# A two-layer decoder trunk: norm ratio in two parts, a third gate pair plain, the scan's first blocks moved up, the residual added later

## The chip, the core and the metric

The kernel runs on one core of one Trainium2 chip. The metric is the device time of one execution in microseconds (us). The engines are TensorE (PE; its weight loads are PEld), VectorE (DVE), ScalarE (ACT) and GpSimd (POOL); SyncE (SP) issues most transfers and ScalarE the stores of intermediate tensors.

## The reference, cut to what is computed

All is float32: 1024 positions plus 16 meta tokens, width 1024.

```python
h = concat([meta, x])                                     # 1040 x 1024
h = h + mixer_rglru_swa(rmsnorm(h, g0))                   # layer 0: recurrence and window attention
h = h + swiglu(rmsnorm(h, f0), w_gu0, w_down0)
q, k, v, g = split(rmsnorm(h, g1) @ ret_w_in)             # layer 1: retention, 4 heads
for block in blocks:                                      # 9 blocks of 128 positions per head
    o = (q_b @ k_b.T * decay) @ v_b + (q_b * dq) @ state
    state = decay_chunk * state + (k_b * dk).T @ v_b
h = h + (silu(g) * rmsnorm_noaffine(o)) @ ret_w_out
h = h + swiglu(rmsnorm(h, f1), w_gu1, w_down1)
# swiglu: gate, up = split(x @ w_gu); (silu(gate) * up) @ w_down;  d_ff = 2816
```

## The kernel before

**Products.** Each factor is a pair of parts, a rounded high part and the rest. For the moving operand the high part is an ACT cast (`oh`, L782) and the low part a subtraction (`ol`, L783) on DVE or POOL; for weights these are `hi` (L111, ACT) and `lo` (L113). `mm3` issues three matmuls for a product (high by high L160, high by low and low by high L161 and L162). A matrix product works on pairs of 128-wide blocks: `seven` does a 2 by 2 product of blocks in seven block products, for which POOL forms four sums of weight blocks (`S`, L145 to L151) and DVE four differences of the moving blocks (`T`, L777, in `mixed`). `eight` does it plainly, with eight block products and no sums or differences. In layer 0 a product is 520 wide in two chunks of 260; in layer 1 it is 512 wide, for keys and values 520.

**Norms.** The normed input is needed as two halves of the positions (hf 0 and 1). A half's scale is `ratio`: two DVE scalings, five small matmuls with a column of ones (L276) for the mean, a power, DVE diagonals (`dg`, L284), small matmuls that spread them over the partitions (L285) and an ACT copy. It multiplies the products after the matmul, so the matmuls can start before it. All of `ratio` is emitted in one piece.

**The feed-forward part (`ffn`).** It has 11 pairs of 256 columns. For each, a gate product and an up product; pair 0 is done by `eight`, the rest by `seven`. The differences of the input (`late[1]`) are made during pair 0. Each pair's result is stored in seven tensors `hd` by DMAs that ACT issues (L883). Then come the down products, in groups of pairs: 2, 3, 2, 2, 2 in layer 0 and 2, 3, 3, 3 in layer 1. A group loads `hd` (L894), casts it, and does four `seven` (mp 0 to 3), whose results DVE adds onto h (L828). Before group 0's products the residual h is read back from DRAM (`residual`, L752: 16 tiles), and all additions go onto it. The `ol` of a group's first pair is on DVE in group 0, the rest on POOL, and in later groups all of them are on POOL.

**Retention.** The input projection has 24 products of 256 columns: gate pairs 0 and 1 by `eight` (`first8`; `ratio` for both halves is called in pair 0), 4 key and query pairs, 8 value pairs, then gate pairs 2 to 7 by `seven`. Between gate pairs 6 and 7, block 0 of head 0 is prepared (`ahead`: loads, value parts, key transposes L1195). The scan then goes over 36 blocks: `updates`, `ahead` one block further, `outputs`, `state`, and `third` (gating of the block before: `yt`, `yh`). Output products of a half head (`output`) are put between blocks as fills. After the last head's output the residual gets its new value (L1285), and is normed (L762), stored and split for layer 1's feed-forward part.

**Order.** Operations go to the engines in the order that a scheduler makes of the emission order, and each engine takes its own in order. 56 SBUF buffers (`slot`), 18 more (`xslot`, `fslot`, `rslot`) and 8 PSUM banks (`ps` 4, `ax` 4) are handed out as they come free.

Of the kernel before, what the change touches and what calls it, by code (L numbers as in the profile page):

```python
# [71 lines left out]
def tile_hybrid(ctx: ExitStack, tc, hT, wfm, wqkv, wo0, lruw, pk, qkg, ck, c0, ret_tab, ret_m,  # L72
# [193 lines left out]
    def ratio(acc, n, sc, pool):  # L266

# [12 lines left out]
        for c0 in range(0, len(cols), 4):  # L280
            ps = bank()
            for j, (a, w) in enumerate(cols[c0:c0 + 4]):
                dg = stg.tile([P, P], F32, tag="dg", bufs=5, name=nm("dg"))
                nc.vector.tensor_scalar(dg[:w, :w], ident[:w, :w], rc[:w, c0 + j:c0 + j + 1], None, op0=ALU.mult)  # L284
                nc.tensor.matmul(ps[:, j * P:j * P + w], ones[:w, :], dg[:w, :w], start=True, stop=True)  # L285
            a, b = cols[c0][0], min(n, cols[c0][0] + 512)
            nc.scalar.copy(R[:, a:b], ps[:, :b - a])
        return R[:, :n]
# [512 lines left out]
    def eight(u, xs, chunks, evac):  # L801

        last = None
        for m, c in ((1, 1), (2, 1), (1, 2), (2, 2)):
# [5 lines left out]
            if last:  # L810
                evac(*last)
            last = (m, c, [ps[:, :b - a] for ps, (a, b) in zip(bk, chunks)])
        evac(*last)
# [3 lines left out]
    def ffn(fp, wgu, wd, groups, xs, R, n, late, done):  # L817
# [13 lines left out]
        for i in range(NP):  # L831
# [27 lines left out]
            if i == 0:  # L859
                def gate0(m, c, bk):  # L860
                    if (m, c) == (1, 2):
                        R.append(late[0]())
# [9 lines left out]
                eight(unit4(wgu[0]), xs, chunks, gate0)  # L872
                late[1](0, 1)
                eight(unit4(wgu[NP]), xs, chunks, up0)
                late[1](2, 3)
            else:
                seven(unit22(wgu[i], 512, fp), xs, chunks, blocks(gt))
                seven(unit22(wgu[NP + i], 512, fp), xs, chunks, blocks(ut))
# [5 lines left out]
        def residual(mp):  # L884
            for m in (2 * mp, 2 * mp + 1):
                for hf in range(2):
                    h[m][hf] = unspill(m, hf, n, xslot if hf and m >= 4 else None)

        for gi, grp in enumerate(groups):
            xs = [{} for _ in grp]  # L890
            for ki, key in enumerate(MOVING):
                for j, i in enumerate(grp):
                    raw = xslot("raw")[:, :n]
                    nc.sync.dma_start(raw, hd[i][key])  # L894
                    xs[j][key] = hilo(raw, n, slot, nc.gpsimd if gi or j else nc.vector)
                if gi == 0 and ki == 1:
                    residual(0)
            w = len(grp) * P
            for mp in range(4):
                if gi == 0 and mp < 3:  # L900
                    residual(mp + 1)
                h1, h2 = h[2 * mp], h[2 * mp + 1]
                outs = (h1[0], h1[0], h1[1], h2[1], h2[1], h1[1], h2[0])

                def evac(k, bk):
                    each(add, outs[k], bk, outs[k])
# [547 lines left out]
```

## Time and profile before

| | us |
|---|---|
| median of three runs (range) | 2714.45 (2713.97 to 2720.88) |
| the profiled execution | 2718.94 |
| its span, first to last instruction | 2717.2 |
| TensorE busy | 2588.8 |
| VectorE busy | 1819.7 |
| GpSimd busy | 1491.8 |
| ScalarE busy | 1153.4 |

The profiled execution is one of its own; its time is the span and 1.7 us around it. Times in the rows count from the start of the span. A granted clock of 1.00 is TensorE's 2.4 GHz and 0.50 is 1.2 GHz; a stretch in between is a mean of the two. A window's PE busy time is the length less the time in which no matmul ran, whatever the clock. "A <- B" in a list of waits means that A's engine sat idle until B's instruction ended.

### The profile page before, as it was taken

The numbers are of one execution on the slowest core, as the hardware profiler recorded it, in microseconds if no ns is written. First come the engines' busy times: TensorE is split into PE (matmuls) and PEld (weight loads), VectorE is DVE, ScalarE is ACT, GpSimd is POOL, SyncE is SP. The second block draws the span as 40 slices with busy tenths as digits, with TensorE's granted clock in tenths as the row PEclk, the third lists the DMA queues.
The fourth block names the chain that finished last, engine by engine and source line by source line (L and its number), as shares of the span: only waits on it lengthen the run. The fifth ranks groups of instructions, "written<-read, shape, count | busy, mean of one in ns | idle before, by whom it ended". The sixth has DMA issues, their size and how long they took to land.

```text
span 2717.2 us, 43283 instructions
## 1 busy us (share of the span) xinstructions
PE 2588.8 (95%) x15734; PEld 2287.1 (84%) x15734; DVE 1819.7 (67%) x3130; ACT 1153.4 (42%) x2425; POOL 1491.8 (55%) x1358
## 2 busy tenths in 40 slices
PE   8989999999998999889999997999989999998999
PEld 7877989999998999779899875777767788886777
DVE  6977676666666889878844344555588655556875
ACT  4666543333333444332233444555543333334442
POOL 3746234554554867457754444454454655565784
PEclk9999999999999999999999998999999999999999
DMA  4001141223225643323232334343332232226442
GB/s 151 32 27 54 63 165 61 96 102 111 84 105 178 207 123 94 113 78 110 98 102 95 117 107 169 114 134 115 106 128 79 96 112 102 97 93 232 161 150 89
DMA packets 145318, 302.31 MB, mean 111 GB/s; under 512 B 18512, under 2 KB 35408, under 8 KB 145104
## 3 DMA queue, kind: packets, MB, share of 16 engines
q1 hardware_dynamic: 103792, 232.49, 25.6%
q10 hardware_dynamic: 41152, 66.54, 6.6%
q8 instruction: 123, 2.02, 0.3%
q14 instruction: 91, 0.75, 0.1%
q0 software_dynamic: 160, 0.52, 0.1%
HBM read 216.60 MB, written 82.89 MB: 110 GB/s over the span
## 4 chain that ended last, share of the span: by engine, by line
PE 78%; DVE 12%; ACT 3%; issue 3%; POOL 2%; DMA 1%; ACTq 0%; SPq 0%; DVEq 0%; POOLq 0%
PE ps L160 16%; PE ps L162 16%; PE ps L161 16%; PE ax L160 8%; PE ax L161 8%; PE ax L162 8%; DVE lo L113 3%; DVE ol L783 1%; DVE h L828 1%; DVE T L777 1%; PE ps L673 1%; DVE xp L762 1%; POOL ol L783 1%; PE ps L1097 1%; ACT oh L782 1%
## 5 line engine op out<-in xcount | busy, mean ns | idle before, releaser
L160 PE MATMUL ps<-oh,hi 128*128 128x260 f32 (+1 forms) x2160 | 695.2, 324 | 20.9 <-ACT oh L782 10.3
L162 PE MATMUL ps<-oh,lo 128*128 128x260 f32 (+1 forms) x2160 | 691.5, 323 | 12.8 <-DVE lo L113 12.6
L161 PE MATMUL ps<-ol,hi 128*128 128x260 f32 (+1 forms) x2160 | 694.0, 322 | 0.5 <-DVE ol L783 0.5
L160 PE MATMUL ax<-oh,hi 128*128 128x260 f32 (+1 forms) x1652 | 531.1, 324 | 9.5 <-ACT oh L782 3.8
L161 PE MATMUL ax<-ol,hi 128*128 128x260 f32 (+1 forms) x1652 | 532.1, 323 | 5.3 <-DVE ol L783 5.3
L162 PE MATMUL ax<-oh,lo 128*128 128x260 f32 (+1 forms) x1652 | 527.7, 322 | 0.9 <-DVE lo L113 0.9
L113 DVE TENSOR_TENSOR lo<-S,hi 128x512 fp32r<-128x512 f32 (+2 forms) x392 | 342.3, 876 | 212.8 <-ACT hi L111 197.9
L111 ACT CAST hi<-S 128x512 fp32r<-128x512 f32 (+2 forms) x392 | 219.0, 561 | 567.3 <-PE ps L161 251.3
L160 PEld LDWEIGHTS ps<-oh,hi 128*128 128x128 f32 x2160 | 409.4, 190 | 58.7 <-ACT oh L782 11.4
L162 PEld LDWEIGHTS ps<-oh,lo 128*128 128x128 f32 x2160 | 408.4, 190 | 49.3 <-DVE lo L113 16.9
L161 PEld LDWEIGHTS ps<-ol,hi 128*128 128x128 f32 x2160 | 410.4, 190 | 32.9 <-DVE ol L783 1.3
L291 POOL TENSOR_TENSOR t<-t,rf 128x520 f32<-128x520 f32 (+1 forms) x190 | 280.4, 1483 | 118.8 <-DVE t L1027 47.3
L160 PEld LDWEIGHTS ax<-oh,hi 128*128 128x128 f32 x1652 | 313.2, 190 | 37.9 <-ACT oh L782 4.7
L161 PEld LDWEIGHTS ax<-ol,hi 128*128 128x128 f32 x1652 | 313.3, 190 | 31.8 <-DVE ol L783 6.8
L113 DVE TENSOR_TENSOR lo<-raw,hi 128x512 fp32r<-128x512 f32 (+2 forms) x312 | 266.7, 858 | 106.0 <-ACT hi L111 99.1
L162 PEld LDWEIGHTS ax<-oh,lo 128*128 128x128 f32 x1652 | 312.2, 189 | 26.7 <-DVE lo L113 1.6
L111 ACT CAST hi<-raw 128x512 fp32r<-128x512 f32 (+2 forms) x344 | 199.4, 584 | 311.9 <-PE ps L161 188.9
L145 POOL TENSOR_TENSOR S<-rb 128x512 f32<-128x512 f32 (+2 forms) x98 | 115.8, 1182 | 317.5 <-DVE lo L113 286.8
L783 POOL TENSOR_TENSOR ol<-raw,oh 128x520 fp32r<-128x520 f32 (+1 forms) x140 | 202.2, 1471 | 24.5 <-ACT oh L782 10.3
L151 POOL TENSOR_TENSOR S<-raw,S 128x512 f32<-128x512 f32 (+2 forms) x98 | 130.8, 1335 | 80.2 <-DVE lo L113 77.4
L146 POOL TENSOR_TENSOR S<-S,raw 128x512 f32<-128x512 f32 (+2 forms) x98 | 116.0, 1183 | 83.3 <-issue 49.3
L149 POOL TENSOR_TENSOR S<-raw,rb 128x512 f32<-128x512 f32 (+2 forms) x98 | 122.7, 1252 | 52.0 <-DVE lo L113 52.0
(303 smaller groups left out, 4773.6 us busy)
## 6 DMA issues: line engine op xcount, KB each, us to landing
raw<-in_wgu_dram SPq DMA_DIRECT2D x48, 512.0 KB, 3.3
rb<-in_wgu_dram SPq DMA_DIRECT2D x40, 512.0 KB, 3.2
raw<-hd SPq DMA_DIRECT2D x77, 260.0 KB, 3.4
raw<-hd SPq DMA_DIRECT2D x77, 256.0 KB, 3.0
raw<-in_wro_dram SPq DMA_DIRECT2D x32, 512.0 KB, 3.3
raw<-in_wr_dram SPq DMA_DIRECT2D x26, 512.0 KB, 3.3
hd<-T ACTq DMA_DIRECT2D x44, 260.0 KB, 2.7
rb<-in_wr_dram SPq DMA_DIRECT2D x22, 512.0 KB, 3.4
```

Source lines behind the costliest of these rows:

```text
L111: nc.scalar.copy(hi, src)
L113: eng.tensor_tensor(out=lo, in0=src, in1=f32(hi), op=ALU.subtract)
L145: nc.gpsimd.tensor_tensor(out=s1, in0=a21, in1=a22, op=ALU.add)
L146: nc.gpsimd.tensor_tensor(out=s2, in0=s1, in1=a11, op=ALU.subtract)
L149: nc.gpsimd.tensor_tensor(out=s3, in0=a11, in1=a21, op=ALU.subtract)
L151: nc.gpsimd.tensor_tensor(out=s4, in0=a12, in1=s2, op=ALU.subtract)
L160: nc.tensor.matmul(ps, ah, bh, start=first and i == 0, stop=False, skip_group_check=more)
L161: nc.tensor.matmul(ps, ah, bl, start=False, stop=False, skip_group_check=more)
L162: nc.tensor.matmul(ps, al, bh, start=False, stop=last and i == n - 1, skip_group_check=more)
L291: (eng or nc.vector).tensor_tensor(out=out_, in0=a, in1=b, op=ALU.mult)
L673: nc.tensor.matmul(k.po[:n, o:o + 64], sb[:, i * P:(i + 1) * P], vt[:, k.b - len(segs) + 1 + j, g * 64:(g + 1) * 64], start=False, stop=g ...
L783: eng.tensor_tensor(out=lo, in0=src, in1=f32(hi), op=ALU.subtract)
```

## The change

The norm ratio is cut in two: `ratio_begin` (scalings, means, power) returns `finish` (diagonals, their matmuls, the copy). `eight` takes hooks that run behind a given block, and with hooks it holds two blocks back before it evicts, not one. The feed-forward part's gate pair 1 in both layers, and gate pair 2 of retention, go by `eight`. In the down products, group 0's first product onto each h tile is copied by ACT and the others are added, with no residual; the residual is loaded into temporaries and added by DVE behind mp 1 to 3 of group 1 and mp 0 of group 2. The `ol` of every group's first pair is on DVE. In retention, `ahead` works two blocks further; blocks 0 to 2 of head 0 are emitted before gate pair 7, and what depends on the gates follows behind block 4. The norm of the last head's half 0 is put off until the last block's gating is emitted.

```diff
     def ratio(acc, n, sc, pool):
+        return ratio_begin(acc, n, sc, pool)()
+    def ratio_begin(acc, n, sc, pool):
...
-        for c0 in range(0, len(cols), 4):
-            ps = bank()
-            for j, (a, w) in enumerate(cols[c0:c0 + 4]):
-                dg = stg.tile([P, P], F32, tag="dg", bufs=5, name=nm("dg"))
-                nc.vector.tensor_scalar(dg[:w, :w], ident[:w, :w], rc[:w, c0 + j:c0 + j + 1], None, op0=ALU.mult)
-                nc.tensor.matmul(ps[:, j * P:j * P + w], ones[:w, :], dg[:w, :w], start=True, stop=True)
-            a, b = cols[c0][0], min(n, cols[c0][0] + 512)
-            nc.scalar.copy(R[:, a:b], ps[:, :b - a])
-        return R[:, :n]
+        def finish():
+            for c0 in range(0, len(cols), 4):
+                ps = bank()
+                for j, (a, w) in enumerate(cols[c0:c0 + 4]):
+                    dg = stg.tile([P, P], F32, tag="dg", bufs=5, name=nm("dg"))
+                    nc.vector.tensor_scalar(dg[:w, :w], ident[:w, :w], rc[:w, c0 + j:c0 + j + 1], None, op0=ALU.mult)
+                    nc.tensor.matmul(ps[:, j * P:j * P + w], ones[:w, :], dg[:w, :w], start=True, stop=True)
+                a, b = cols[c0][0], min(n, cols[c0][0] + 512)
+                nc.scalar.copy(R[:, a:b], ps[:, :b - a])
+            return R[:, :n]
+        return finish
...
-    def eight(u, xs, chunks, evac):
-        last = None
-        for m, c in ((1, 1), (2, 1), (1, 2), (2, 2)):
+    def eight(u, xs, chunks, evac, hooks={}):
+        wait = []
+        for i, (m, c) in enumerate(((1, 1), (2, 1), (1, 2), (2, 2))):
...
-            if last:
-                evac(*last)
-            last = (m, c, [ps[:, :b - a] for ps, (a, b) in zip(bk, chunks)])
-        evac(*last)
+            if i in hooks:
+                hooks[i]()
+            wait.append((m, c, [ps[:, :b - a] for ps, (a, b) in zip(bk, chunks)]))
+            if len(wait) > (2 if hooks else 1):
+                evac(*wait.pop(0))
+        for w in wait:
+            evac(*w)
...
-            if i == 0:
-                def gate0(m, c, bk):
-                    if (m, c) == (1, 2):
-                        R.append(late[0]())
+            if i < 2:
+                def gate0(m, c, bk, gt=gt):
...
-                eight(unit4(wgu[0]), xs, chunks, gate0)
+            if i == 0:
+                fin = []
+                eight(unit4(wgu[0]), xs, chunks, gate0,
+                      {2: lambda: fin.append(late[0]()), 3: lambda: R.append(fin[0]())})
...
+            elif i == 1:
+                eight(unit4(wgu[i]), xs, chunks, gate0)
...
+            if i:
...
         def residual(mp):
...
-                    h[m][hf] = unspill(m, hf, n, xslot if hf and m >= 4 else None)
+                    t = unspill(m, hf, n)
+                    nc.vector.tensor_tensor(out=h[m][hf][:, :n], in0=h[m][hf][:, :n], in1=t[:, :n], op=ALU.add)
...
         for gi, grp in enumerate(groups):
...
-                    xs[j][key] = hilo(raw, n, slot, nc.gpsimd if gi or j else nc.vector)
-                if gi == 0 and ki == 1:
-                    residual(0)
+                    xs[j][key] = hilo(raw, n, slot, nc.vector if j == 0 else nc.gpsimd)
...
-                if gi == 0 and mp < 3:
-                    residual(mp + 1)
-                h1, h2 = h[2 * mp], h[2 * mp + 1]
-                outs = (h1[0], h1[0], h1[1], h2[1], h2[1], h1[1], h2[0])
+                at = [(2 * mp + r, c) for r, c in ((0, 0), (0, 0), (0, 1), (1, 1), (1, 1), (0, 1), (1, 0))]
...
-                    each(add, outs[k], bk, outs[k])
+                    m, hf = at[k]
+                    if gi == 0 and k in (0, 2, 3, 6):
+                        h[m][hf] = xslot("h") if hf and m >= 4 else slot("h")
+                        each(lambda o, ps: nc.scalar.copy(o, ps), h[m][hf], bk)
+                    else:
+                        each(add, h[m][hf], bk, h[m][hf])
...
                 seven(unit22(wd[gi][mp], w, fp), xs, chunks, evac)
+                if gi == 1 and mp or gi == 2 and not mp:
+                    residual((mp - 1) % 4)
...
     def late0():
-        r = ratio(acc[1], 520, sc[1], fp)
-        products((Rf[0], r), sc)
-        return r
+        finish = ratio_begin(acc[1], 520, sc[1], fp)
+        def run():
+            r = finish()
+            products((Rf[0], r), sc)
+            return r
+        return run
...
-        pend = []
+        pend, temps = [], [slot]
...
-                    t[key] = slot("t")
+                    t[key] = temps[0]("t")
...
         def scaled(chunks, c, t, bk):
...
-                t = slot("t")
+                t = temps[0]("t")
...
         def first8(i, between):
...
-            def evac(m, c, bk):
-                if m == 1 and i == 0:
-                    Rr.append(ratio(acc2[c - 1], 520, tr[c - 1], ap))
-                fin(m - 1, c - 1, None, bk)
-            eight(unit4(wr[8 + i]), xo2, REST, evac)
+            part = []
+            def begin(c):
+                part.append(ratio_begin(acc2[c], 520, tr[c], ap))
+            def end():
+                Rr.append(part.pop(0)())
+            def turn():
+                end()
+                begin(1)
+            eight(unit4(wr[8 + i]), xo2, REST, lambda m, c, bk: fin(m - 1, c - 1, None, bk),
+                  {1: lambda: begin(0), 2: turn, 3: end} if i == 0 else {})
...
+        first8(2, ())
...
-        for i in range(2, 7):
+        for i in range(3, 7):
...
+        def turn(i):
+            k, b = seq[i]
+            if b < 8:
+                updates(k, b)
+            ahead(i + 2)
+            if b:
+                outputs(k, b)
+            if b < 8:
+                state(k, b)
         ahead(0)
+        ahead(1)
+        for i in range(3):
+            turn(i)
+        temps[0] = aslot
         proj7(15, REST, gate(7))
...
+        tail = []
...
         def output(hd, hf, u_, yh, yl):
...
                 if hd == NH - 1:
-                    if m == 0:
-                        acc3[hf] = slot("acc")
-                    xp[m][hf] = normed(m, hf, "g3", 512, tr[hf][:, 8:520], acc3[hf])
-                    spill(m, hf, 0, 512)
-                    plain(xo, xp, m, hf, 512, slot, nc.vector)
+                    def run(m=m):
+                        if m == 0:
+                            acc3[hf] = slot("acc")
+                        xp[m][hf] = normed(m, hf, "g3", 512, tr[hf][:, 8:520], acc3[hf])
+                        spill(m, hf, 0, 512)
+                        plain(xo, xp, m, hf, 512, slot, nc.vector)
+                    tail.append(run)
+                    while hf and tail:
+                        tail.pop(0)()
...
         for i, (k, b) in enumerate(seq):
-            if b < 8:
-                updates(k, b)
-            ahead(i + 1)
-            if b:
-                outputs(k, b)
-            if b < 8:
-                state(k, b)
-            if i and seq[i - 1][1]:
-                third(*seq[i - 1])
-                if seq[i - 1][1] in (4, 8):
-                    k_, hf = seq[i - 1][0], seq[i - 1][1] // 8
-                    fills += [(lambda k_=k_, hf=hf, u_=u_: output(k_.hd, hf, u_, *k_.ys[hf])) for u_ in range(4)]
-            if i == 4:
+            if i > 2:
+                turn(i)
+            for k_, b_ in seq[1:4] if i == 4 else seq[i - 1:i] if i > 4 else ():
+                if not b_:
+                    continue
+                third(k_, b_)
+                if b_ in (4, 8):
+                    fills += [(lambda k_=k_, hf=b_ // 8, u_=u_: output(k_.hd, hf, u_, *k_.ys[hf])) for u_ in range(4)]
+            if i == 5:
...
-            if fills and i not in (32, 33):
+            if fills and i not in (32, 33, 34):
...
+        while tail:
+            tail.pop(0)()
...
-    late = (lambda: ratio(acc3[1], 512, tr[1][:, 8:520], fp), mixes(xo, xp, 512, lambda j: fslot if j < 2 else slot))
+    late = (lambda: ratio_begin(acc3[1], 512, tr[1][:, 8:520], fp), mixes(xo, xp, 512, lambda j: fslot if j < 2 else slot))
```

On TensorE, in retention's gate pair 0, the second half's means stand behind the first half's ratio. Before, the rows from its means (L276) to its diagonals' matmuls (L285) are:

```order
L276 MATMUL ax_14649<-ckt,acc_13748 128x1 x4
L276 MATMUL ax_14649<-ckt,acc_13748 8x1
L160 MATMUL ps_14974<-oh_13744,hi_14942 128x260
L161 MATMUL ps_14974<-ol_13745,hi_14942 128x260
...
L162 MATMUL ps_14974<-oh_14307,lo_14944 128x260
L285 MATMUL ax_14659<-dg_14660,ckt 128x128
L285 MATMUL ax_14659<-dg_14663,ckt 128x128
```

In the kernel after, where `finish` is a function of its own, the same place reads (L280 for the means, L291 for the diagonals):

```order
L291 MATMUL ax_14636<-dg_14637,ckt 128x8
L280 MATMUL ax_14645<-ckt,acc_13777 128x1 x4
L280 MATMUL ax_14645<-ckt,acc_13777 8x1
L160 MATMUL ax_14659<-oh_13783,hi_14525 128x512
L161 MATMUL ax_14659<-ol_13784,hi_14525 128x512
...
L162 MATMUL ps_14983<-oh_13794,lo_14971 128x512
L291 MATMUL ax_14684<-dg_14685,ckt 128x128
L291 MATMUL ax_14684<-dg_14688,ckt 128x128
```

Between the means and the diagonals stood 12 matmuls of 260 columns; now there are 30 of 512 columns.

In SP's queue, at layer 0's first group of down products (`raw` from `hd` is a load of a group, `h` from `keep` one of the residual), it was:

```order
L894 DMA raw_10708<-hd_5626 128x520
L894 DMA raw_10714<-hd_6126 128x520
L752 DMA h_10874<-keep_1913_4854 128x520
L752 DMA h_10878<-keep_1924_4901 128x520
L752 DMA h_11026<-keep_1935_4948 128x520
L752 DMA h_11030<-keep_1946_4995 128x520
L894 DMA raw_11320<-hd_6614 128x520
L894 DMA raw_11326<-hd_7114 128x520
L752 DMA h_10652<-keep_0806_4487 128x520
L752 DMA h_10654<-keep_1859_4633 128x520
L752 DMA h_10656<-keep_0811_4498 128x520
L752 DMA h_10658<-keep_1880_4713 128x520
```

It is now:

```order
L911 DMA raw_10697<-hd_5626 128x520
L911 DMA raw_10703<-hd_6123 128x520
L141 DMA rb_11006<-in_wd_0_dram 128x512
...
L911 DMA raw_11301<-hd_6611 128x520
...
L911 DMA raw_12255<-hd_8119 128x520
L760 DMA h_11799<-keep_0806_4487 128x520
L760 DMA h_11802<-keep_1859_4633 128x520
L911 DMA raw_12261<-hd_8619 128x520
```

The residual's loads have moved from within the loads of group 0 and 1 to behind the loads of group 1 and among those of group 2.

On DVE, at the last head's last block (`yt` is the gating of that block, `xp` and `ol` from it a normed tile of half 0), the rows were:

```order
L762 SCALAR_TENSOR_TENSOR xp_23181<-h_20101,pkt,R_14734 128x512
L1285 TENSOR_TENSOR h_20103<-ps_23202,h_20103 128x512
L783 TENSOR_TENSOR ol_23189<-xp_23181,oh_23188 128x512
L762 SCALAR_TENSOR_TENSOR xp_23216<-h_20103,pkt,R_14734 128x512
L1285 TENSOR_TENSOR h_20105<-ps_23227,h_20105 128x512
L783 TENSOR_TENSOR ol_23224<-xp_23216,oh_23223 128x512
L762 SCALAR_TENSOR_TENSOR xp_23241<-h_20105,pkt,R_14734 128x512
L1285 TENSOR_TENSOR h_20107<-ps_23271,h_20107 128x512
L783 TENSOR_TENSOR ol_23249<-xp_23241,oh_23248 128x512
L291 TENSOR_TENSOR yt_23257<-ax_23252,sg_22969 128x512
```

They are now:

```order
L1332 TENSOR_TENSOR h_20213<-ps_23151,h_20213 128x512
L113 TENSOR_TENSOR lo_23345<-raw_23337,hi_23343 128x512
L1332 TENSOR_TENSOR h_20215<-ps_23184,h_20215 128x512
L299 TENSOR_TENSOR yt_23170<-ax_23165,sg_23005 128x512
L770 SCALAR_TENSOR_TENSOR xp_23251<-h_20207,pkt,R_14763 128x512
L1332 TENSOR_TENSOR h_20217<-ps_23198,h_20217 128x512
L791 TENSOR_TENSOR ol_23257<-xp_23251,oh_23256 128x512
L770 SCALAR_TENSOR_TENSOR xp_23260<-h_20209,pkt,R_14763 128x512
L1332 TENSOR_TENSOR h_20219<-ps_23222,h_20219 128x512
```

The last block's `yt` stands ahead of the first normed tile, where it stood behind six of them.

## Rows read from the trace of the kernel before

**Rows 1.** The page's head, then its busy times: busy us, share, instructions.

```profile
span 2717.2 us, 43283 instructions
...
PE 2588.8 (95%) x15734; PEld 2287.1 (84%) x15734; DVE 1819.7 (67%) x3130; ACT 1153.4 (42%) x2425; POOL 1491.8 (55%) x1358
```

**Rows 2.** The page's chain that ended last, by engine.

```profile
PE 78%; DVE 12%; ACT 3%; issue 3%; POOL 2%; DMA 1%; ACTq 0%; SPq 0%; DVEq 0%; POOLq 0%
```

**Rows 3.** Windows: stretch, length, each engine's busy us (instructions), granted clock, DMA share, GB/s.

```profile
440.00:480.00 40.00, 34.90 (x256) 34.10 (x255) 35.06 (x49) 15.59 (x31) 21.16 (x13) 0.87 0.23 81
520.00:840.00 320.00, 320.00 (x2668) 320.00 (x2667) 206.15 (x295) 118.58 (x239) 165.44 (x119) 1.00 0.27 98
840.00:920.00 80.00, 69.70 (x537) 67.96 (x536) 60.58 (x112) 34.57 (x74) 48.09 (x41) 0.94 0.67 231
920.00:1080.00 160.00, 155.62 (x1288) 154.52 (x1287) 138.34 (x285) 66.10 (x144) 121.86 (x109) 1.00 0.40 118
1120.00:1240.00 120.00, 105.23 (x571) 90.08 (x570) 93.88 (x125) 41.81 (x79) 65.66 (x47) 0.94 0.26 91
1600.00:1720.00 120.00, 103.78 (x437) 80.29 (x436) 57.15 (x101) 57.63 (x126) 53.01 (x57) 0.93 0.44 150
2000.00:2040.00 40.00, 31.67 (x132) 24.96 (x132) 35.47 (x43) 16.07 (x30) 19.36 (x14) 0.87 0.38 138
2080.00:2120.00 40.00, 35.28 (x136) 26.58 (x135) 33.97 (x42) 15.60 (x28) 21.85 (x15) 0.91 0.26 93
2120.00:2440.00 320.00, 320.00 (x1380) 258.87 (x1379) 183.57 (x239) 114.75 (x200) 176.16 (x125) 1.00 0.29 102
2440.00:2560.00 120.00, 110.81 (x456) 85.99 (x455) 90.51 (x125) 50.88 (x102) 84.77 (x67) 0.97 0.62 210
```

**Rows 4.** TensorE's waits, 440 to 520: who waits for whom, total us, times, longest.

```profile
PE ax L161 <- DVE ol L783: 2.7, 1, 2.7
PE ps L162 <- DVE lo L113: 1.6, 1, 1.6
```

**Rows 5.** TensorE's waits, 840 to 920.

```profile
PE ps L160 <- ACT oh L782: 6.1, 1, 6.1
PE ps L160 <- DVE h L828: 2.0, 1, 2.0
```

**Rows 6.** Timeline, 865 to 873: start, us, engine, line, operation, idle before and its end.

```profile
865.04 5.00 SPq L752 DMA_DIRECT2D h<-keep  x4
...
871.65 1.68 ACT L782 CAST oh<-raw 128x520 fp32r<-128x520 f32 x3 [4.72 <-DMA h<-keep]
```

**Rows 7.** TensorE's waits, 1120 to 1240.

```profile
PE ax L285 <- DVE dg L284: 6.1, 2, 3.4
...
PE ps L162 <- DVE lo L113: 4.8, 2, 3.5
...
PE ax L160 <- ACT oh L782: 2.3, 1, 2.3
```

**Rows 8.** TensorE's waits, 1600 to 1720.

```profile
PE ax L160 <- ACT kd L1195: 12.5, 6, 5.9
```

**Rows 9.** Timeline, 2000 to 2010, around the last block of the scan.

```profile
2007.36 0.68 DVE L291 TENSOR_TENSOR yt<-ax,sg 128x512 f32<-128x512 f32 x1
...
2008.85 1.65 PE L160 MATMUL ps<-yh,hi 128*128 128x512 f32 x3 [6.75 <-ACT yh L1248]
```

**Rows 10.** TensorE's waits, 2440 to 2560.

```profile
PE ps L160 <- ACT oh L782: 4.3, 2, 3.4
```

**Rows 11.** Tile h on VectorE, 860 to 1110: count, duration ns min/median/max.

```profile
L828 DVE TENSOR_TENSOR h<-ps,h x153: 409/416/430, 880.7 to 1109.6; 128x260 f32<-128x260 f32 x153
```

**Rows 12.** Tile lo on VectorE, 920 to 1080.

```profile
L113 DVE TENSOR_TENSOR lo<-S,hi x56: 408/558/1664, 919.5 to 1079.8; 128x256 fp32r<-128x256 f32 x40, 128x384 fp32r<-128x384 f32 x16
```

**Rows 13.** Tile ol on VectorE, 440 to 480.

```profile
L783 DVE TENSOR_TENSOR ol<-T,oh x12: 686/692/1822, 441.2 to 470.9; 128x520 fp32r<-128x520 f32 x12
```

**Rows 14.** Tile ol on GpSimd, 900 to 1060.

```profile
L783 POOL TENSOR_TENSOR ol<-raw,oh x52: 1288/1490/1644, 899.4 to 1058.2; 128x520 fp32r<-128x520 f32 x52
```

## The prediction

> **What bounds the kernel now.** I read the busy times first: TensorE is busy for 2588.8 of 2717.2 us [rows 1], and in the chain that ended last it has 78%, DVE 12%, ACT 3% [rows 2]. So the time is TensorE's work plus what it loses, and a change pays only where TensorE waits or runs slowly. Next I read the windows [rows 3]. In undisturbed stretches TensorE does 2668 matmuls of 260 columns in 320 us (0.120 us each) and 1380 of 512 in 320 us (0.232 us each), at a granted clock of 1.00. The lost time is in a few stretches. For each I count the idle time (length less PE busy) and the clock's loss: at a mean granted clock c in a window W, the slow part runs at 1.2 instead of 2.4 GHz, and half of its length is lost, which makes (1-c)W. From rows 3:
>
> - 440 to 480 (layer 0, gate pair 1): 5.1 idle + 0.13x40 = 5.2, so 10.3.
> - 840 to 920 (layer 0, start of the down products): 10.3 + 4.8 = 15.1.
> - 1120 to 1240 (start of retention): 14.8 + 7.2 = 22.0.
> - 1600 to 1720 (start of the scan): 16.2 + 8.4 = 24.6.
> - 2000 to 2040 (the last block): 8.3 + 5.2 = 13.5.
> - 2080 to 2120 (layer 1, gate pair 1): 4.7 + 3.6 = 8.3.
> - 2440 to 2560 (layer 1, start of the down products): 9.2 + 3.6 = 12.8.
>
> Together 106.6 us. In each of these windows the clock is below 1.00 where TensorE had just been idle, so a wait that goes takes its slow stretch along. Last I read who ends the waits in these stretches [rows 4 to 10], and what DVE's and GpSimd's instructions cost [rows 11 to 14].
>
> **What it costs TensorE.** Three products by `eight` instead of `seven` mean one more block product each: 24 matmuls of 260 columns in layer 0, 12 of 512 in retention, 12 of 512 in layer 1. 24x0.120 + 24x0.232 = +8.5 us [rows 3]. Nothing hides these. The two-part ratio, the moved blocks and the late residual add no matmul.
>
> **Gate pair 1, layer 0.** TensorE waits 2.7 us for an `ol` of a difference T and 1.6 us for a `lo` behind it in DVE's queue [rows 4], with DVE busy 35.1 of 40 us [rows 3]. A plain product needs no T: its 192 matmuls (23 us) stand between, and the first T is needed two block products into the up product. Against it: the last four T take their buffers only when the plain product has let go of its own, so that some 5.7 us (48 matmuls) remain for them. I take -8 of the 10.3 (ends 0 and -10.3).
>
> **Layer 1, gate pair 1.** The same with 96 matmuls of 0.232: -7 of 8.3 (ends 0 and -8.3).
>
> **Start of retention.** The wait for the diagonals is 6.1 us in two pieces, the longer 3.4 [rows 7]. The second half's ratio had 12x0.120 = 1.4 us of matmuls to hide behind and gets 30x0.232 = 7.0, so its 2.7 goes. The first half's cover stays (18 matmuls instead of 21), and so does its 3.4. Gate pair 2 by `eight` puts 22 us between the differences T and their first use, so the 3.5 of the 4.8 for `lo` and the 2.3 for `oh` go [rows 7]. With half of the clock's 7.2: -2.7 - 3.5 - 2.3 - 3.6 = -12 (ends -2.7 and -18).
>
> **Start of the scan.** Six waits for `kd`, the scaled keys, make 12.5 us, one of them 5.9 [rows 8]: with one block of look-ahead, block b's chain of loads, transposes and ACT copies isn't done when TensorE asks for it. Now gate pair 7's 84 matmuls (19.5 us) lie among the first blocks' chains. I take two thirds of the waits and half of the 8.4 for the clock: -8 - 4 = -12 (ends 0, if the value loads are late all the same, and -21). For the rest of the scan I take nothing.
>
> **The last block.** TensorE waits 6.75 us for `yh`, ready when `yt` was run by DVE at 2007.36 [rows 9], behind six normed tiles in DVE's queue. They now come later. The normed work isn't gone: it stands beside half 1's 96 output matmuls (22 us), and the plain products of half 0 cover half 1's tiles. -7 of 13.5 (ends +3, if half 1's tiles are then late, and -12).
>
> **First group of the down products.** The wait of 6.1 us is for the first cast of a `raw` [rows 5], which ACT did at 871.65 when transfers of h<-keep had kept its queue waiting for 4.72 us; SP issued the first four at 865.04 [rows 6], in a window where the DMA engines are 0.67 busy [rows 3]. Without these loads I take half of the wait, since the stores of the last pair and the `raw` loads themselves stay: -3. The 2.0 for DVE's h [rows 5] goes, as ACT writes four of seven results. With half of the clock's 4.8: -7.5 (ends -2 and -13). In layer 1, 4.3 us of waits for the same cast [rows 10] fall to 1.5, and half of 3.6 goes: -4.5, of which +1 is given back as below: -3.5.
>
> **Groups 1 and 2, DVE.** This is where the change costs. DVE is busy 138.3 of 160 us there, 34.6 in the 40.3 us (336 matmuls) of a group of two pairs [rows 3]. It gets 7 `ol` more per group, 12 additions of the residual in group 1 and 4 in group 2. The trace has no such addition; the nearest row is `ol` on DVE, 0.69 to 1.82 us, median 0.69 [rows 13], of the same 520 columns and two SBUF inputs. The `lo` subtractions show why it spreads, 0.41 to 1.66 [rows 12], while additions that read PSUM keep to 0.41 to 0.43 [rows 11]: two inputs from SBUF are slow beside GpSimd's work. GpSimd loses 7x1.49 = 10.4 us per group [rows 14], so I take 1.0 us each. Group 1 (three pairs, 60.5 us): 1.5x34.6 + 19 = 71 us. Group 2: 34.6 + 11 = 45.6. Groups 3 and 4: 41.6. That is 10.5 + 5.3 + 2x1.3 = 18 us over TensorE's pace. Some 24 `lo` per group get shorter as GpSimd does less, about 0.1 us each, which takes back 2.4 to 3.6 per group, some 11. I take +6 in layer 0 (ends 0 and +20), and +1 in layer 1, where DVE is busy 90.5 of 120.
>
> **Sum.** What goes: -8 - 7 - 12 - 12 - 7 - 7.5 - 3.5 = -57. Of this I hold back an eighth, as DVE ends 12% of the chain [rows 2] and takes the next place when a wait goes: +7. With +6 and +8.5: -35.5. The profiled execution took 2718.9 us (span and 1.7 around it), 4.5 more than the median of the runs, 2714.45; I put the difference onto the median: 2679.
>
> **Rivals.**
>
> First, the waits at the scan's start and the last block only move: the value loads and DVE's normed tiles are still late by as much. For it: `kd` waits stand behind loads, and DVE is busy 35.5 of 40 us around the last block [rows 3]. Against it: ACT is busy 57.6 of 120 us at the scan's start, so there is room to work ahead. -12 - 7 are then missing: 2698.
>
> Second, slower: DVE bounds the down products. 32 additions and 49 moved `ol` come to DVE. At 1.5 us each, near the upper end of rows 13, the 44 of layer 0 take 66 us with 26 us of room (60.5 - 51.9 and three times 5.7), so 40 over; the 37 of layer 1 take 55 with about 40 of room (58.5 us of matmuls in a group, DVE busy 0.75 of them, three groups), so 15 over. 55 in the place of 7 makes 2679 + 48 = 2727. It decides from about 1.3 us each. For it: DVE's 0.86 share; against it, GpSimd's own load falls.
>
> Third, DVE and GpSimd take turns at one resource, so moving `ol` off GpSimd gives more than it takes: a group of two pairs now has GpSimd's 121.9/4 = 30.5 us and 28 `lo` of 0.41, 42 us of turns in 40.3. In group 2 this becomes 30.5 - 10.4 + 11.5 + 11x0.69 = 39.2. Then the +6 goes and so do some 4 us of small waits there: 2669. The Trainium skill ("GPSIMD Engine Reference", Key points) says that GpSimd shares its SBUF interfaces with VectorE, with contention where a DVE instruction has two SBUF inputs; the trace agrees in the spread of `lo` (0.41 to 1.66) beside additions from PSUM (0.41 to 0.43), but doesn't show whether the two take turns or only slow down. By it alone the time would be 2669.
>
> **How the numbers follow.** The forecast 0.60, with its own range 2660 to 2697; the first rival 0.17; the second 0.10; the third 0.13. A measurement of this kernel can tell about 0.3% (8 us) from no change, so faster means below 2706, and slower above 2722. Faster: 0.57 of the forecast's 0.60, 0.13 of the third rival, 0.11 of the first rival, so 0.81. No change: 0.03 + 0.05 = 0.08. Slower: the second rival and 0.01 of the first, 0.11. The range reaches from 2655 to 2712: some 0.05 are left out below and 0.12 above.
>
> **What would show it.** Right: PE's waits at 440 to 480 and in layer 1's gate pair 1 are gone and the clock is 1.00 there; one wait for diagonals at the start of retention, not two; the wait for `yh` of the last block below 1 us; the first cast of the down products waits for no h. Wrong: waits for `kd` at the scan's start of 8 us or more; DVE busy above 39 of 40 us in groups 1 and 2 with waits of TensorE for h of over 8 us per layer; additions of the residual at 1.3 us or more; the plain products at more than 8.5 us.

## The result and the profile after

The kernel after takes 2698.96 us in the median of its runs, the kernel before 2714.82: a ratio of 0.9938, with an interval of 0.9917 to 0.9959. One of its five runs took 4956 us, in a slow state, and is left out of the ratio. The change is 16 us less where 35.5 were forecast. The profiled execution of the kernel after has a span of 2703.4 us, 13.8 less than before. The page's head, busy times (engine, us, share, instructions) and chain:

```profile
span 2703.4 us, 43322 instructions
PE 2593.5 (96%) x15782; PEld 2296.1 (85%) x15782; DVE 1841.3 (68%) x3154; ACT 1160.5 (43%) x2452; POOL 1404.4 (52%) x1288
...
PE 79%; DVE 12%; ACT 3%; issue 3%; DMA 2%; POOL 1%; SPq 0%; ACTq 0%; DVEq 0%; POOLq 0%
```

TensorE's busy time is up by 4.7 us [rows 1], for 48 matmuls more, and the span is down: less is lost. DVE keeps its 12% of the chain [rows 2]. The windows (stretch, length, busy us of PE, PEld, DVE, ACT, POOL with instructions, granted clock, DMA share, GB/s) are moved to where each stage now lies, and answer to [rows 3]:

```profile
440.00:480.00 40.00, 40.00 (x335) 40.00 (x335) 33.79 (x50) 12.98 (x24) 17.89 (x11) 1.00 0.20 74
836.00:916.00 80.00, 73.36 (x578) 72.10 (x576) 51.67 (x90) 37.53 (x94) 37.65 (x34) 0.96 0.38 122
916.00:1076.00 160.00, 146.53 (x1141) 143.21 (x1139) 146.49 (x281) 68.92 (x145) 93.77 (x80) 0.96 0.51 165
1132.00:1252.00 120.00, 118.66 (x657) 101.57 (x655) 101.00 (x133) 47.03 (x88) 66.48 (x46) 1.00 0.30 108
1593.00:1713.00 120.00, 104.23 (x445) 80.44 (x444) 57.81 (x103) 59.47 (x129) 53.68 (x60) 0.94 0.46 156
1988.00:2028.00 40.00, 39.30 (x177) 31.77 (x176) 36.47 (x46) 17.53 (x32) 19.42 (x13) 1.00 0.35 128
2055.00:2095.00 40.00, 39.70 (x171) 31.84 (x170) 39.76 (x48) 14.68 (x27) 22.80 (x14) 1.00 0.26 93
2410.00:2530.00 120.00, 106.50 (x427) 82.30 (x427) 74.58 (x105) 55.95 (x114) 65.38 (x54) 0.94 0.48 160
```

Reading them as in the prediction (idle time plus (1-c)W): gate pair 1 of layer 0 loses 0 us (was 10.3), the start of retention 1.3 (was 22.0), the scan's start 15.8 + 7.2 = 23.0 (was 24.6), the last block 0.7 (was 13.5), layer 1's gate pair 1 0.3 (was 8.3). The two starts of the down products lose 6.6 + 3.2 = 9.8 (was 15.1) and 13.5 + 7.2 = 20.7 (was 12.8), and the groups behind the first, 916 to 1076, 13.5 + 6.4 = 19.9, where they lost 4.4. TensorE's waits in the whole of layer 0's down products (waiting, waited for, total us, times, longest), of which [rows 5] shows the start, first before (840 to 1126), then after (836 to 1131):

```profile
PE ps L160 <- ACT oh L782: 6.1, 1, 6.1
PE ps L160 <- DVE h L828: 5.0, 5, 2.0
```

```profile
PE ps L160 <- DVE h L840: 10.6, 9, 3.5
PE ax L161 <- DVE ol L791: 3.1, 2, 2.3
PE ps L160 <- ACT oh L790: 2.9, 1, 2.9
```

The first wait for a cast has fallen from 6.1 to 2.9 us as forecast, but the waits for DVE's h have gone from 5.0 to 10.6, and there are 3.1 for `ol`. In layer 1 the waits for the cast, forecast to fall from 4.3 [rows 10] to 1.5, haven't fallen (2410 to 2530):

```profile
PE ps L160 <- ACT oh L790: 4.8, 2, 3.4
```

From one stage's landmark to the next (the last store of a pair, the last addition of a layer's down products, the first addition of an output product), the two profiles differ by -3.9 us up to the down products of layer 0, +15.4 in these, -18.3 up to the first output product, -23.3 from there to the end of layer 1's gate products, and +16.2 in layer 1's down products. So the question was why the down products cost 31 us where -5 was forecast, and why the rest gave 45 where 31 was forecast.

### The profile page after: what moved, and what is told of

It is laid out like the page before. It is cut to its first block, busy times and chain, and to the rows that moved or that the text cites. A ratio compares the mean times of both kernels' runs of the same rounds, so it can differ in the third digit from the quotient of the medians.

```text
span 2703.4 us, 43322 instructions
## 1 busy us (share of the span) xinstructions
PE 2593.5 (96%) x15782; PEld 2296.1 (85%) x15782; DVE 1841.3 (68%) x3154; ACT 1160.5 (43%) x2452; POOL 1404.4 (52%) x1288
## 4 chain that ended last, share of the span: by engine, by line
PE 79%; DVE 12%; ACT 3%; issue 3%; DMA 2%; POOL 1%; SPq 0%; ACTq 0%; DVEq 0%; POOLq 0%
PE ps L160 16%; PE ps L161 16%; PE ps L162 16%; PE ax L160 9%; PE ax L161 9%; PE ax L162 9%; DVE lo L113 2%; DVE ol L791 2%; DVE xp L770 1%; DVE h L840 1%; PE ps L681 1%; DMA raw<-hd 1%; DVE T L785 1%; PE ps L1120 1%; DMA h<-keep 1%
## 5 line engine op out<-in xcount | busy, mean ns | idle before, releaser
L113 DVE TENSOR_TENSOR lo<-S,hi 128x512 fp32r<-128x512 f32 (+2 forms) x380 | 314.1, 828 | 194.8 <-ACT hi L111 181.7
L162 PEld LDWEIGHTS ps<-oh,lo 128*128 128x128 f32 x2160 | 409.1, 190 | 42.0 <-DVE lo L113 10.4
L111 ACT CAST hi<-S 128x512 fp32r<-128x512 f32 (+2 forms) x380 | 212.0, 559 | 523.7 <-PE ps L161 263.8
L113 DVE TENSOR_TENSOR lo<-raw,hi 128x512 fp32r<-128x512 f32 (+2 forms) x318 | 257.4, 813 | 108.3 <-ACT hi L111 100.2
L299 POOL TENSOR_TENSOR t<-t,rf 128x520 f32<-128x520 f32 (+1 forms) x181 | 267.6, 1486 | 112.8 <-DVE t L1050 48.5
L791 POOL TENSOR_TENSOR ol<-raw,oh 128x512 fp32r<-128x512 f32 (+1 forms) x91 | 143.0, 1594 | 19.9 <-ACT oh L790 8.5
```

The source lines that it names most:

```text
L111: nc.scalar.copy(hi, src)
L113: eng.tensor_tensor(out=lo, in0=src, in1=f32(hi), op=ALU.subtract)
L162: nc.tensor.matmul(ps, al, bh, start=False, stop=last and i == n - 1, skip_group_check=more)
L299: (eng or nc.vector).tensor_tensor(out=out_, in0=a, in1=b, op=ALU.mult)
L791: eng.tensor_tensor(out=lo, in0=src, in1=f32(hi), op=ALU.subtract)
```

## The experiments

All times are medians beside runs of the kernel before on the same chip (2716 to 2720 us); a difference under some 4 us between two of them is not told apart.

**The down products alone, both ways.** `e_down_back` is the kernel after with `ffn`'s part from `residual` to the group loop as before; `e_down_alone` is the kernel before with that part as after.

```diff
...
+                if gi == 0 and mp < 3:
+                    residual(mp + 1)
...
-                if gi == 1 and mp or gi == 2 and not mp:
-                    residual((mp - 1) % 4)
```

> The kernel after, with the down products (residual, first products, ol) as in the kernel before. Theory A (the down products cost what was not forecast: +15 us in layer 0 and +16 in layer 1 in the two profiles): 2699 - 31 = 2668 (2660 to 2676). Rival B (the down products only show a delay that comes from elsewhere, such as a later first load): 2690 to 2700.

> The kernel before, with only the down products changed. Theory A: slower by the same 31 us, 2746 (2735 to 2755). Rival B: 2710 to 2720.

Measured: 2663.8 (ratio 0.9811, 0.9796 to 0.9825) and 2742.4 (1.0098, 1.0079 to 1.0116). The down products cost 35 us in the kernel after and 26 in the kernel before. Theory A stands, and `e_down_back` beats both kernels.

**The parts of it.** `e_ol_back` has one line of that part as before, `e_res_back` all of it but that line:

```diff
-                    xs[j][key] = hilo(raw, n, slot, nc.vector if j == 0 else nc.gpsimd)
+                    xs[j][key] = hilo(raw, n, slot, nc.gpsimd if gi or j else nc.vector)
```

> The kernel after, with only the ol of groups 1 and up on GpSimd again (the late residual stays). Theory A1 (VectorE's load in groups 1 and 2 is what costs, the ol with 28 x 1.16 + 21 x 1.26 = 59 us being more of it than the 32 additions with 30 us): 2699 - 18 = 2681 (2675 to 2688). Rival A2 (the additions cost, since they stand in VectorE's queue and wait for their loads): 2694 to 2702. Third theory (VectorE and GpSimd take turns, so that ol on GpSimd is dearer): 2702 to 2715.

> The kernel after, with the residual loaded ahead of group 0 and all results added on VectorE as before, but the ol of every group's first pair on VectorE as after. Theory A1: the ol still cost about 18 and group 0's waits come back: 2685 (2678 to 2692). Rival A2 (the additions and their loads are the cost): 2668 to 2676.

Measured: 2694.6 and 2688.6. The first lies in A2's range and the second in A1's, so neither theory holds alone: the one half gives back 4.4 of the 35, the other 10.3. The other way round, `e_res_back` differs from `e_down_back` by `ol` on VectorE alone, and that costs 24.9 us (2688.6 - 2663.8). TensorE's waits for VectorE in layer 0's down products (860 to 1130), in `e_down_back` and in `e_res_back`:

```profile
PE ps L160 <- DVE h L840: 5.0, 5, 2.0
```

```profile
PE ps L160 <- DVE h L840: 13.1, 11, 2.6
```

So the price of a part depends on what else is in the kernel.

`e_no_res` is the kernel after without the call of `residual`, `e_no_res_ol` without that and with the `ol` line as before:

> The kernel after without the residual in both feed-forward parts (loads and 32 additions are left out, so the output lacks it); the ol stay on VectorE. It shows what the additions and their loads cost where they now stand. Theory A1 (VectorE's queue is the bound in groups 1 and 2): 2699 - 20 = 2679 (2670 to 2686), since the ol alone still cost 10 to 15. Rival A3 (the copies by ScalarE in group 0 are the cost, as they delay its casts): 2692 to 2700.

> The kernel after with the ol on GpSimd in groups 1 and up, and without the residual in both feed-forward parts (loads and 32 additions left out, so the output lacks it). What is left of the change in the down products is ScalarE's copies in group 0 and the loads that are gone from it. Theory A1 (VectorE's extra work is all that costs): faster than the kernel after with the down products as before (2663.8), by group 0's waits for the residual: 2655 (2650 to 2660). Rival A3 (ScalarE's copies delay its casts and hold PSUM, by 5 us or more per layer): 2668 to 2680.

Measured: 2686.6 and 2676.0. Against `e_down_back`, which has the residual, a kernel that leaves it out and has its `ol` on GpSimd is still 12 us slower. The `ol` on VectorE then add 10.5. (2686.6 lies 0.6 above A1's range, 2676.0 in that of A3, which the next run tests.) TensorE's waits in layer 0's down products, first in `e_no_res_ol`, then in `e_no_res`:

```profile
PE ps L161 <- POOL ol L791: 3.3, 2, 2.4
PE ps L160 <- DVE h L840: 3.1, 5, 1.3
```

```profile
PE ps L160 <- DVE h L840: 9.8, 8, 1.9
```

With the `ol` on VectorE, TensorE waits 9.8 us for VectorE's results instead of 3.1.

**Where the 12 us are.** `e_copy_dve` is `e_no_res_ol` with group 0's copies by VectorE:

```diff
-                        each(lambda o, ps: nc.scalar.copy(o, ps), h[m][hf], bk)
+                        each(lambda o, ps: nc.vector.tensor_copy(o, ps), h[m][hf], bk)
```

> The kernel with the ol on GpSimd in groups 1 and up and without the residual (2676.0 measured; the output lacks the residual), with group 0's first products copied by VectorE instead of ScalarE. Theory A3 (ScalarE's copies stand in its queue among the casts and hold PSUM): 2664 (2658 to 2668), since VectorE is then as it was in group 0 with the additions. Rival A5 (what costs is that the loads of group 1 come at another time): 2673 to 2680.

Measured: 2677.5. So ScalarE's copies are not the cause. What remained was the transfers. Loads of `hd` issued by SP in the 60 us from the start of layer 1's group 0, in the kernel before and in the kernel after (count: ns of an issue, first and last start):

```profile
L894 SPq DMA_DIRECT2D raw<-hd x34: 319/320/1144, 2489.8 to 2547.5; - x34
```

```profile
L911 SPq DMA_DIRECT2D raw<-hd x23: 319/383/608, 2500.0 to 2518.9; - x23
```

Before, group 1's loads are issued from the start of group 0; after, none is issued in its first 41 us, and 23 come within 19 us around its end. In the kernel after an h tile takes its buffer at its first write, which is late in group 0, and by theory A6 group 1's loads, which come behind it in the program, are ordered behind it. `e_claim_nores` changes only that moment in `e_no_res_ol`, by a first write of one column on GpSimd; `e_claim_ol` does the same in `e_ol_back`, with the residual:

```diff
+            if gi == 0:
+                for m in range(KD):
+                    for hf in range(2):
+                        h[m][hf] = xslot("h") if hf and m >= 4 else slot("h")
+                        nc.gpsimd.memset(h[m][hf][:, 0:1], 0.0)
             w = len(grp) * P
...
-                        h[m][hf] = xslot("h") if hf and m >= 4 else slot("h")
```

> The kernel with the ol on GpSimd in groups 1 and up and without the residual (2676.0 measured; the output lacks the residual), with a one-column memset by GpSimd of each of the 16 h tiles ahead of group 0's products, so that the tiles take their buffers there. Theory A6 (a tile takes its buffer at its first write, and group 1's loads, which come later in the program, stand behind the last h tile's: they are issued 42 us into group 0 of layer 1 in the trace, instead of from its start): the 12 us go, 2662 (2655 to 2667). Rival A3 (the copies themselves): 2672 to 2680.

> The same memset in the kernel with the ol on GpSimd and the late residual (2694.6 measured); nothing is left out. Theory A6: 12 us go and the late additions with their loads still cost some 18: 2682 (2675 to 2687). If the additions only cost where group 1's loads were late: 2662 to 2672.

Measured: 2658.2 and 2674.8, so 18 and 20 us less where 12 were expected of each. The first lies in A6's range, the second 0.2 us below its lower end of 2675; theory A6 is shown. The loads in `e_claim_nores`, and the windows of three times 20 us from the end of layer 1's gate products in `e_no_res_ol` and then `e_claim_nores`:

```profile
L911 SPq DMA_DIRECT2D raw<-hd x34: 319/320/383, 2432.8 to 2489.3; - x34
```

```profile
2440.00:2460.00 20.00, 17.99 (x64) 13.14 (x64) 16.03 (x20) 12.41 (x28) 13.79 (x11) 0.85 0.22 66
2460.00:2480.00 20.00, 18.77 (x82) 14.86 (x80) 10.51 (x20) 10.23 (x24) 7.05 (x8) 1.00 0.28 79
2480.00:2500.00 20.00, 15.17 (x49) 10.93 (x49) 7.53 (x11) 12.99 (x27) 14.23 (x12) 0.83 0.88 297
```

```profile
2432.00:2452.00 20.00, 16.91 (x55) 12.22 (x56) 16.57 (x20) 14.87 (x32) 16.73 (x25) 0.83 0.79 252
2452.00:2472.00 20.00, 20.00 (x88) 16.20 (x87) 15.43 (x21) 14.11 (x32) 18.62 (x16) 1.00 0.57 178
2472.00:2492.00 20.00, 20.00 (x88) 16.25 (x87) 14.89 (x17) 11.59 (x24) 20.00 (x16) 1.00 0.66 202
```

In the first, GpSimd is 7.1 of 20 us busy in the middle, without an `ol`, and eight `ol` come at the end (10.4 of its 14.2 us), with PE busy 15.2 of 20 and a clock of 0.83. In the second, GpSimd works evenly (18.6, 20.0), and in these two stretches TensorE doesn't stop.

**The additions.** Three other ways to do them: by GpSimd (`e_res_pool`, in the kernel after), two behind each mp of groups 1 and 2 (`e_res_spread`, in the kernel after), and, in `e_ol_back`, with temporaries in `xslot` (`e_res_xslot`) or loads issued by GpSimd (`e_res_queue`).

```diff
-                    nc.vector.tensor_tensor(out=h[m][hf][:, :n], in0=h[m][hf][:, :n], in1=t[:, :n], op=ALU.add)
+                    nc.gpsimd.tensor_tensor(out=h[m][hf][:, :n], in0=h[m][hf][:, :n], in1=t[:, :n], op=ALU.add)
...
+            for m in (mp,):
...
-                    residual((mp - 1) % 4)
+                    residual(4 * (gi - 1) + mp)
...
-                    t = unspill(m, hf, n)
+                    t = unspill(m, hf, n, xslot)
...
+                    t = slot("h")
+                    nc.gpsimd.dma_start(t[:, :n], kept[m, hf])
```

> The kernel after with the 32 additions of the residual on GpSimd instead of VectorE. Theory A1 (time in VectorE's queue): 30 us of VectorE's work go, 2683 (2676 to 2690). Rival A2 (late loads and the order behind them, whichever engine adds): 2695 to 2705. Third theory (the two engines take turns, so it does not matter who adds, and GpSimd is dearer): 2700 to 2712.

> The kernel after with the additions spread: two behind each mp of groups 1 and 2 instead of four behind mp 1 to 3 of group 1 and mp 0 of group 2. Theory A1 by total load (VectorE over its pace in groups 1 and 2 together): 2692 to 2702, since group 2 of layer 0 has less room. Theory A1 by bursts (four additions in a row, 4 us, hold up the release of PSUM): 2684 to 2691.

> The kernel with the ol on GpSimd and the late residual (2694.6 measured), with the residual's temporaries in the 18 buffers of the raw loads instead of the 56 common ones. Theory A4 (the temporaries and the next group's parts compete for the common buffers, so that loads stand behind them): 2680 to 2688. Theory A1 (the additions' place in VectorE's queue): 2691 to 2698.

> The kernel with the ol on GpSimd and the late residual (2694.6 measured), with the residual's loads issued by GpSimd instead of SyncE. Theory A2 (the loads are late, as they stand in SyncE's queue behind and among the next group's loads, and hold up VectorE by 8 us in layer 1 and the loads behind them): 2680 to 2688. Theory A1: 2691 to 2700, as the issues cost GpSimd time.

Measured: 2700.7, 2698.0, 2694.4 and 2708.3. None helps, and the last costs 14. The first lies in the ranges of A2 and of the third theory, the second in that of total load, the third in A1's, the last in none. With the buffers claimed early the additions still cost 2674.8 - 2658.2 = 16.6. VectorE's additions in `e_claim_ol`, 911 to 1035 (count, busy, mean ns, idle before and its end):

```profile
L904 DVE TENSOR_TENSOR h<-h,h 128x520 f32<-128x520 f32 x16 | 17.9, 1117 | 4.4 <-DMA h<-keep 4.4
```

They take 17.9 us in layer 0, and VectorE stands 4.4 us more in front of them for their loads. Since it makes no difference which engine adds, I can't say how the cost divides between the adding and the loads; that stays open. One candidate is weak: ScalarE's casts wait 20.1 us for these additions in `e_ol_back` and not at all in `e_res_xslot`, which is no faster (2694.4 against 2694.6).

**The other parts**, each taken back in `e_down_back`: `e_plain_back` (the three gate pairs by `seven`), `e_gate2_back` (retention's pair 2 by `seven` only), `e_ratio_back` (the ratio in one piece, one block held), `e_scan_back` (look-ahead, first blocks and last norm as before), `e_ahead_back` (look-ahead and first blocks only).

```diff
-        first8(2, ())
...
-        for i in range(3, 7):
+        for i in range(2, 7):
...
-            ahead(i + 2)
+            ahead(i + 1)
...
-        ahead(1)
-        for i in range(3):
-            turn(i)
```

> The kernel after with the down products as before (2663.8 measured for that) and the three gate pairs (pair 1 in both layers, pair 2 of retention) by seven products again. Theory from the prediction's terms: the stalls of 8 + 7 + part of 12 us come back and 8.5 us of matmuls go: 2663.8 + 12 = 2676 (2670 to 2681). Rival (the plain products only cost, and the other parts took the waits away): 2655 to 2662.

> The kernel after with the down products as before (2663.8) and only retention's gate pair 2 by seven products again; pair 1 stays plain in both layers. By the prediction's term (5.8 of waits and half of the clock's 7.2, less 2.8 of matmuls): 2670 (2667 to 2674). By the ledger of the kernel without plain pairs (retention 25 us longer up to the first output): 2688 (2682 to 2692).

> The kernel after with the down products as before (2663.8) and the norm ratio in one piece everywhere, one block held back. By the prediction's term (2.7 for the second diagonals and some clock): 2668 (2665 to 2672). Rival (the plain pair 2 covers what the ratio delays): 2661 to 2665.

> The kernel after with the down products as before (2663.8) and the scan as before: one block of look-ahead, block 0 alone ahead of gate pair 7, the norm of the last head's half 0 at once. By the prediction's terms (12 at the scan's start, 7 at the last block): 2683 (2677 to 2688). Rival (the plain gate pairs alone did it): 2662 to 2670.

> The kernel after with the down products as before (2663.8), the look-ahead of one block and only block 0 ahead of gate pair 7 as before, but the norm of the last head's half 0 still put off. By the prediction's term for the scan's start: 2676 (2671 to 2681). Rival (the waits for the keys only moved, as the first rival said): 2662 to 2668, and the 12 us between the two scans come from the last block.

Measured: 2703.9, 2688.0, 2665.8, 2675.5 and 2667.1. The first lies above both of its ranges and the fourth between its two. So pair 2 plain is worth 24.2 us, pair 1 in both layers 15.9 (2703.9 - 2688.0), the ratio in two parts 2.0 (not told apart from nothing), the last block's norm 8.4 (2675.5 - 2667.1; by the two ratios to the kernel before 5.4), the look-ahead 3.3 (nor is this). Together they make 53.8, near the 53 by which `e_down_back` is faster than the kernel before. The start of retention in `e_gate2_back` and in `e_down_back`:

```profile
1113.00:1233.00 120.00, 105.71 (x552) 90.61 (x552) 90.91 (x123) 42.12 (x78) 64.23 (x45) 0.90 0.25 86
```

```profile
1112.00:1232.00 120.00, 119.40 (x670) 103.34 (x669) 100.28 (x133) 46.93 (x88) 69.60 (x46) 1.00 0.31 110
```

Without the plain pair the stretch loses 14.3 us idle and 12.0 by a clock of 0.90; with it 0.6. Layer 1's gate pair 1 in `e_plain_back`, by `seven`, and in `e_gate2_back`, plain:

```profile
2070.00:2110.00 40.00, 30.43 (x104) 21.77 (x104) 28.80 (x39) 14.22 (x26) 24.59 (x14) 0.87 0.27 92
```

```profile
2068.00:2108.00 40.00, 38.64 (x165) 30.49 (x164) 36.23 (x46) 15.76 (x29) 20.75 (x14) 1.00 0.30 106
```

It loses 9.6 + 5.2 = 14.8 us against 1.4. In the kernel before, by `seven` too but with the last norm at its old place, it lost 8.3 [rows 3]. The waits for keys in `e_ahead_back` at the scan's start:

```profile
PE ax L160 <- ACT kd L1223: 11.1, 6, 5.7
```

and those of TensorE in the kernel after, which answer to [rows 8]:

```profile
PE ps L160 <- ACT yh L1279: 2.9, 1, 2.9
PE ax L160 <- ACT kd L1226: 2.2, 1, 2.2
PE ps L160 <- ACT t L1047: 2.0, 2, 1.1
PE ax L1209 <- DVE kd L1227: 1.9, 1, 1.9
PE ax L160 <- DVE kd L1227: 1.6, 1, 1.6
PE ax L1209 <- DMA qf<-qd: 1.5, 1, 1.5
```

Six waits for one instruction, 11.1 us, have become seven for several others, 12.1 us. From 1575 to 1700 all of TensorE's waits are 14.8 us in `e_ahead_back` and 14.5 in `e_down_back`, which differs from it by this part alone.

## Why the prediction was wrong

The step that failed is "First group of the down products" together with "Groups 1 and 2, DVE": -7.5 - 3.5 + 6 (and +1 within the 3.5), -5 in all, where the runs have +35 in the kernel after. That 2699 comes out 1 us from the first rival's 2698 is luck: the rival lacks the last block's gain, which came, and has the down products as forecast. They missed by 40, and the other parts made up for 22 of it.

- The first group's wait did fall (6.1 to 2.9). What I left out is what the same edit does to the next group's loads: late loads cost 18 us (2676.0 - 2658.2). It could be read beforehand. The rows of SP's order that I had quoted show it: before, group 1's loads (`raw_11320`) follow group 0's and four loads of the residual; after, its first (`raw_11301`) stands behind weight loads, the first of which is quoted. I read in them only that the residual's loads had moved. In layer 1 the cast's wait, put at -2.8, gave nothing (4.3 before, 4.8 after).
- The additions and the `ol` took the durations that I had estimated as 1.0 us. VectorE's rows in the kernel after, 917 to 1040 (count, busy, mean ns, idle before and its end):

```profile
L791 DVE TENSOR_TENSOR ol<-raw,oh 128x520 fp32r<-128x520 f32 x22 | 25.5, 1161 | 0.8 <-ACT oh L790 0.8
...
L904 DVE TENSOR_TENSOR h<-h,h 128x520 f32<-128x520 f32 x16 | 15.3, 954 | 1.9 <-DMA h<-keep 1.9
```

Additions 0.95 us and `ol` 1.16, where `ol` had 0.69 as the median [rows 13]. The 11 us for shorter `lo` came too. The `lo` of sums of weights, 256 wide, in `e_down_back` (915 to 1060) and, with only the `ol` moved, in `e_res_back` (915 to 1070):

```profile
L113 DVE TENSOR_TENSOR lo<-S,hi 128x256 fp32r<-128x256 f32 x33 | 27.4, 838 | 1.9 <-ACT hi L111 1.9
```

```profile
L113 DVE TENSOR_TENSOR lo<-S,hi 128x256 fp32r<-128x256 f32 x32 | 18.5, 582 | 0.0
```

All `lo` there take 69.2 us in `e_down_back` (83 of them) and 53.3 in `e_res_back` (82). So they give back 16 of the 25.8 us that 22 `ol` cost, and still layer 0's down products are 14.5 us longer (253.8 and 268.3 between the landmarks). The error was in what VectorE has room for: I counted a group's total against TensorE's pace, while TensorE stops when a result is late, and slow stretches follow (the granted clock of 916 to 1076 is 0.96, of 920 to 1080 before 1.00). Taken one after the other from `e_claim_nores`, the pieces are: late loads +17.8, `ol` on VectorE +10.5, additions +12.4; the sum, 40.8, less the 5.6 us by which `e_claim_nores` (without a residual) is faster than `e_down_back`, is 35. Another order gives other pieces, as the 24.9 for `ol` in `e_res_back` shows.
- The second rival, slower by VectorE's load in the down products, had the right place and the right sign for them. Its price, 55 us, counted additions and `ol`; these made 23 in that order, and the rest of the 35 is another mechanism.
- The third rival, two engines in turns, falls. By it seven `ol` on VectorE would save a group 10.4 - 4.8 = 5.6 us of turns; moving those of both layers costs 10.5 (2686.6 against 2676.0). The Trainium skill ("GPSIMD Engine Reference", Key points) says that GpSimd and VectorE contend where a VectorE instruction has two SBUF inputs. Here this shows in durations (the `lo` above, 0.84 us, and 0.58 with less work on GpSimd), not in a gain from taking work off GpSimd.
- Pair 1 in both layers was forecast at -15 + 5.7 = -9.3 and measured at -15.9, matmuls included, in kernels where layer 1's had 14.8 us to cover and not 8.3. At the start of retention, pair 2 was forecast at -5.8 - 3.6 + 2.8 = -6.6 and gave -24.2. The mechanism was right and the size was off: I let the first diagonals' 3.4 us stay and half of the slow clock, but nearly all of the 22 us of that window went.
- The scan's start was forecast at -12 and gave -3.3, which is the first rival's account of it; the last block at -7 gave -8.4. The second diagonals' wait went, but behind a plain pair 2 the ratio in two parts is worth 2.0, not told apart from nothing.
- The 7 us held back for new waits had no counterpart outside the down products: the other parts together gave 53 us (2716.5 - 2663.8) against 31 forecast for them.

## What to carry to other kernels

A tile that takes its buffer when it is first written can hold back loads that come behind it in the program, here the next group's: when a load is replaced by a late write, look where the next stage's loads stand in the queue, and claim the buffer early. An engine that takes TensorE's results out of PSUM has room only from one result to the next, so its spare time in a window is not a price list. And a plain product that covers the making of operands can be worth more than the waits it names, since the slow clock behind them goes as well.

## What was not expected of the hardware

The slow clock can cost nearly as much as the waits around it: at the start of retention without the plain pair, 14.3 us of idle time come with 12.0 us lost to the clock (0.90 over 120 us), while with it the clock is 1.00.
